# Differential attention: the mean of two softmax maps re-queued, and its outputs summed in PSUM by three products

## The chip, the cores and the metric

The kernel runs as one launch on one core of a Trainium2 chip. The metric is the device time of that core in microseconds (us), lower is better. Five engines work side by side on their own in-order queues: TensorE (PE in the profile, with PEld for its weight loads), VectorE (DVE), ScalarE (ACT), GpSimd (POOL) and SyncE (SP, which here issues DMAs). SBUF is the working memory; PSUM is the accumulation memory that TensorE writes, eight banks of 512 float32 per partition.

## The reference

A decoder trunk of two layers, sequence 512, width 1024, in float32. Layer 0 has differential attention as its token mixer, layer 1 a causal pooling mixer. Around each mixer stand two SwiGLU feed-forward blocks, a cross attention into 256 memory tokens, and a layer norm after each step. Only the differential attention is touched here: 8 heads; each head has two query/key pairs of width 64 and values of width 128. Cut to what matters:

```
for each block of 128 queries i, each head h, each map c in (0, 1):
    s = q[c] @ k[c].T * scale;  s = where(kpos <= qpos, s, min)
    p[c] = softmax(s)
a = p[0] - lam * p[1]
o = a @ v
o = o * rsqrt(mean(o * o) + eps) * subln_g * (1 - lam_init)
y = concat(o over heads) @ w_o
```

## The kernel before

Float32 products are made from rounded halves: an operand x is split into `hi` (x rounded to a shorter format, a cast on ACT) and `lo = x - hi` (a subtraction on DVE), and a product is the sum of hi*hi, hi*lo and lo*hi in one PSUM bank (`mm3`, lines 210 to 212). The trunk runs stage by stage; the projections and feed-forward blocks keep TensorE in such triples.

The differential attention stage has two streams, woven by `weave`. `da_main` is the projections: for each pair of heads the values, then for each head queries and keys (lines 210 to 212 with outputs named v, q, k), with the rotary embedding on DVE and POOL (`da_rope`, L1083 to L1086, output `rt`) and the splits of queries (`qk`, L1096 and L1097) and keys (`qk`, `low`, L1110 to L1112). `da_side` is the attention of heads whose projections are ready, one tile of 128 queries (i = 0..3) of a head at a time. A step s of `da_side` does, for tiles that lag behind each other:

- `da_scores` of tile s: for both maps two products of 128 x 128(i+1) into a bank `sc` (L1125, L1126); then, with priority, on DVE the masked copy `p` and its minimum (L1131, called mask below: one instruction and the read of its accumulator) and on ACT the exponential with its row sum (L1134).
- `da_mix` of tile s-1: on DVE the reciprocal of a row sum (L1143), the factor `cf` (L1144) and `p0 + cf*p1` (L1145), called the mix below. The normalisation of `p0` is left to the end, where the mean square takes it up.
- `da_turn` of tile s-2: transposes of `p` on TensorE (L494, output `pt`), then hi and lo of the result, `a` (L125 on ACT, L126 on DVE).
- `da_out` of tile s-3: the product with the values. For each block j of 128 keys, the hi of `a` is the stationary operand and the hi and lo of the values, side by side, are the moving one (L1166, 256 columns); the lo of `a` meets the hi of the values (L1167, 128 columns). So a bank `po` holds, for two tiles, two sums of 128 columns each that have still to be added: a copy on ACT (L1172), and an addition on DVE (L1173), give `o`. Two Square activations on ACT (L1176) read `o`, and write their elementwise result, which nobody reads, back into the bank `po`; their accumulators are the sums of squares `sq`. After a head's last tile POOL makes the factor `f` (L1183 to L1186), later ACT scales `o` (L1192), TensorE transposes it (L494, `pt<-ident,o`), and it is split into `oT` (L130, L131) for the output projection (`ps`).

The banks for `sc`, `pt` and `po` come in turn from three pools of two (`aux`): a new tile waits until the last reader or writer of the tile that had its bank is done.

The order on each engine is set at build time by a scheduler that takes instructions by priority as their inputs come ready in its own estimate; `high_priority()` lets an instruction go ahead of others, and `after(...)`/`issue_after` places one behind a named instruction in the queue, with no wait on it. On the chip each queue then runs strictly in that order.

Of the kernel before, what the change touches and what calls it, by code (L numbers as in the profile page):

```python
# [12 lines left out]
AF = mybir.ActivationFunctionType  # L13
ALU = mybir.AluOpType
# [3 lines left out]
P = 128  # L18
# [91 lines left out]
class Trunk:  # L110
# [80 lines left out]
    def mm(self, name):  # L191
        return self.mmp.tile([P, S], F32, tag="mm", name=name)
# [922 lines left out]
    def da_scores(self, st, i):  # L1115

        nc = self.nc
        q, k, n = st["q"], st["k"], (i + 1) * P
        qi, kn = slice(i * P, n), slice(0, n)
        mx, rc, cf = self.small("mx"), self.small("rc", (P, 1)), self.small("cf", (P, 1))  # L1120
        sm = st["sm"][:, i]
        sc = [self.aux("sc")[:, :n] for m in range(2)]
        mm = nc.tensor.matmul
        for m in range(2):
            mm(sc[m], q[m][:, qi], k[0][m][:, kn], start=True, stop=False)  # L1125
            mm(sc[m], q[m][:, qi], k[1][m][:, kn], start=False, stop=True)  # L1126
        p = [self.tmp("p")[:, :n] for m in range(2)]
        with self.tc.high_priority():
            for m in range(2):
                least = mx[:, m : m + 1]  # L1130
                nc.vector.tensor_tensor_reduce(  # L1131
                    p[m], sc[m], self.mask[:, S - n :], -1.0, -NEG, ALU.add, ALU.min, least
                )
                nc.scalar.activation(  # L1134
                    p[m], p[m], AF.Exp, bias=least, scale=-1.0, accum_out=sm[:, m : m + 1]
                )
        st["m", i] = p, sm, rc, cf

    def da_mix(self, st, i):

        nc = self.nc
        p, sm, rc, cf = st.pop(("m", i))
        nc.vector.reciprocal(rc, sm[:, 1:2])  # L1143
        nc.vector.scalar_tensor_tensor(cf, sm[:, 0:1], self.nlam, rc, ALU.mult, ALU.mult)  # L1144
        nc.vector.scalar_tensor_tensor(p[0], p[1], cf, p[0], ALU.mult, ALU.add)  # L1145
        st["p", i] = p[0]

    def da_turn(self, st, i):
# [8 lines left out]
    def da_out(self, st, i):  # L1157
        nc = self.nc
        if i == 0:
            st["o"], st["sq"] = self.tmp("o", (P, NT, P)), self.small("sq", (P, NT))  # L1160
        if i % 2 == 0:
            st["po"] = self.aux("po").rearrange("p (i s e) -> p i s e", i=2, s=2)
        a, o, po, mm = st.pop(("a", i)), st["o"], st["po"], nc.tensor.matmul
        for j in range(i + 1):
            v = st["v"][j][:, st["h"] % 2]
            mm(po[:, i % 2], a[0][:, j], v, start=j == 0, stop=False)  # L1166
            mm(po[:, i % 2, 0], a[1][:, j], v[:, 0], start=False, stop=j == i)  # L1167
        if i % 2 == 0:
            return
        o2 = o[:, i - 1 : i + 1]  # L1170
        with self.tc.high_priority():
            nc.scalar.copy(o2, po[:, :, 1])  # L1172
            nc.vector.tensor_tensor(o2, o2, po[:, :, 0], ALU.add)  # L1173
        sq = st["sq"]
        for i in range(i - 1, i + 1):
            nc.scalar.activation(  # L1176
                po[:, 0, 0], o[:, i], AF.Square, scale=float(P**-0.5), accum_out=sq[:, i : i + 1]
            )
        if i < NT - 1:
            return  # L1180

        f, G, s0 = self.small("f", (P, NT)), nc.gpsimd, st["sm"][:, :, 0]
        G.tensor_scalar(f, s0, EPS, None, ALU.mult)  # L1183
        G.tensor_tensor(f, f, s0, ALU.mult)
        G.tensor_tensor(f, f, sq, ALU.add)
        G.tensor_tensor(f, f, self.mhalf, ALU.pow)  # L1186
        st["f"] = f
# [446 lines left out]

    def mixer(self, layer, ln):
        if layer == 0:
            bufs = dict(low=4, rt=2, a=4, p=6, o=2, qk=8, _x=0, v=4, oT=11, mask=1)
            with self.other_pools(), self.phase_pool(("v", "v"), "rt", **bufs):
                self.diff_attention(layer, ln)
            self.close_side()  # L1640
        else:
            self.later = ExitStack()
            self.later.enter_context(self.stage_pools(4, dict(raw=2), ("wh", "wl", "mem", "p", "raw")))
            self.to_w(self.later)
            self.kvp = self.later.enter_context(self.pool("kv"))
            bufs = dict(p=4, pw=1, gb=2, _x=0, pooled=16, sq=1)
            with self.phase_pool(("gb", "gb"), "sq", **bufs):
                side = self.pool_mixer(layer, ln)
                with self.tc.high_priority():
                    self.load_memory()  # L1650
                w = self.a["xa_wkv"][layer]
                raws = [self.raw_cols(w, c) for c in (0, D)]
                self.pool_bias()
                next(side)
                self.kv, self.keys, self.kv_bufs = [], [], 10
                self.weave(self.early_kv(layer, ln, 2, raws), side, 850, 8500)
            self.close_side()
# [46 lines left out]
```

## Time and profile before

| What | Value |
|---|---|
| time, median of 3 runs | 1921.71 us (1919.52 to 1921.93) |
| profiled execution, time and span | 1921.52 us, span 1919.7 us |
| granted TensorE clock, mean | 0.999 |
| busy share of the span | PE 99%, weight loads 91%, DVE 81%, ACT 53%, POOL 17% |
| attention stage, about 355 to 580 us of the span | 225 us: PE busy 217.8, DVE 188.4, ACT 144.9 |

In the trace an output tile and its inputs are written as `out<-in`; `xN` counts instructions. The time behind a bar or in brackets is how long the engine stood idle before the instruction, and for whom it waited. The ends of matmuls are modelled, their starts are recorded, so the cost of a matmul is read best from one start to the next. 128x256 behind a matmul is its output: 128 partitions by 256 columns, the columns being those of the moving operand.

### The profile page before, as it was taken

The page shows a single profiled execution, that of the slowest core. Times are in us where ns is not written, and L with a number is a line of the kernel's source. Part 1 is how long each engine was busy: PE and PEld are TensorE (multiplying, and loading weights), DVE is VectorE, ACT ScalarE, POOL GpSimd, SP SyncE. Part 2 cuts the span into 40 slices and gives each one's busy share as a digit, 9 for nine tenths or more (in the row PEclk, how much of TensorE's full clock was granted, in tenths as well). Part 3 has the DMA queues.
Part 4 walks back from the last instruction along what each step waited for, and adds up shares of the span by engine and source line. Part 5 has one row for each costly group of instructions (what it writes and reads, how often), then busy time and mean ns, then how long its engine had stood idle before and what let it go on. Part 6 is the DMA issues. An engine that isn't in the chain of part 4 may idle for free.

```text
span 1919.7 us, 32489 instructions
## 1 busy us (share of the span) xinstructions
PE 1895.9 (99%) x13072; PEld 1738.2 (91%) x13072; DVE 1563.6 (81%) x2264; ACT 1023.4 (53%) x1580; POOL 319.8 (17%) x278
## 2 busy tenths in 40 slices
PE   9999999999999999999999999999999999999998
PEld 8999998888878888999998999999899889999997
DVE  7888889888867558889888988898787568998886
ACT  6555454567755435645554655455455436555552
POOL 3112121111210002221220311212130012111210
PEclk9999999999999999999999999999999999999999
DMA  9978772322224327987785587878344437877861
GB/s 250 213 173 179 175 140 78 91 66 88 66 88 154 110 66 195 180 179 162 144 192 180 108 180 164 183 164 183 108 132 132 133 87 162 174 168 167 186 133 55
DMA packets 246743, 277.96 MB, mean 145 GB/s; under 512 B 8256, under 2 KB 212544, under 8 KB 246592
## 3 DMA queue, kind: packets, MB, share of 16 engines
q0 software_dynamic: 92928, 92.29, 31.4%
q1 hardware_dynamic: 153664, 183.59, 29.8%
q8 instruction: 103, 1.69, 0.4%
q14 instruction: 48, 0.39, 0.1%
HBM read 273.75 MB, written 2.10 MB: 144 GB/s over the span
## 4 chain that ended last, share of the span: by engine, by line
PE 78%; DVE 13%; ACT 4%; DMA 2%; issue 2%; POOL 1%; SPq 0%; DVEq 0%; ACTq 0%; POOLq 0%
PE x L210 7%; PE x L211 7%; PE x L212 7%; PE z L212 4%; PE z L210 4%; PE z L211 4%; PE ps L210 4%; PE ps L212 4%; PE ps L211 4%; PE px L210 2%; PE px L212 2%; PE px L211 2%; PE y L212 2%; PE xq L210 1%; PE xq L211 1%
## 5 line engine op out<-in xcount | busy, mean ns | idle before, releaser
L685 POOL DMA_DIRECT2D ra<-in_ffn_w_in_dram x132 | 170.7, 1313 | 982.8 <-DVE wl L692 808.9
L690 ACT CAST wh<-ra 128x1024 fp32r<-128x1024 f32 x176 | 185.1, 1054 | 207.5 <-PE x L211 66.5
L692 DVE TENSOR_TENSOR wl<-ra,wh 128x1024 fp32r<-128x1024 f32 x176 | 213.9, 1220 | 67.1 <-ACT wh L690 66.4
L210 PE MATMUL x<-xe,wh 128*128 128x256 f32 x704 | 195.0, 277 | 0.0
L211 PE MATMUL x<-xe,wh 128*128 128x256 f32 x704 | 194.8, 277 | 0.0
L690 ACT CAST wh<-rc 128x1024 fp32r<-128x1024 f32 x132 | 138.9, 1053 | 104.9 <-PE x L211 40.4
L212 PE MATMUL x<-xe,wl 128*128 128x256 f32 x704 | 194.8, 277 | 0.0
L125 ACT CAST wh<-b 128x1024 fp32r<-128x1024 f32 x112 | 117.8, 1052 | 128.9 <-PE x L211 65.1
L692 DVE TENSOR_TENSOR wl<-rc,wh 128x1024 fp32r<-128x1024 f32 x132 | 159.8, 1218 | 26.8 <-ACT wh L690 26.8
L126 DVE TENSOR_TENSOR wl<-b,wh 128x1024 fp32r<-128x1024 f32 x112 | 136.6, 1220 | 40.2 <-ACT wh L125 40.2
L210 PE MATMUL x<-xh,wh 128*128 128x256 f32 x536 | 148.7, 277 | 0.0
L211 PE MATMUL x<-xl,wh 128*128 128x256 f32 x536 | 148.4, 277 | 0.0
L212 PE MATMUL x<-xh,wl 128*128 128x256 f32 x536 | 148.4, 277 | 0.0
L211 PEld LDWEIGHTS x<-xe,wh 128*128 128x128 f32 x704 | 132.5, 188 | 1.4
L210 PEld LDWEIGHTS x<-xe,wh 128*128 128x128 f32 x704 | 132.2, 188 | 1.3
L212 PEld LDWEIGHTS x<-xe,wl 128*128 128x128 f32 x704 | 132.2, 188 | 0.0
L126 DVE TENSOR_TENSOR wl<-raw,wh 128x1024 fp32r<-128x1024 f32 x64 | 83.0, 1300 | 42.4 <-ACT wh L125 41.6
L211 PEld LDWEIGHTS x<-xl,wh 128*128 128x128 f32 x536 | 100.9, 188 | 0.7
L210 PEld LDWEIGHTS x<-xh,wh 128*128 128x128 f32 x536 | 100.6, 188 | 0.7
L212 PEld LDWEIGHTS x<-xh,wl 128*128 128x128 f32 x536 | 100.6, 188 | 0.0
L125 ACT CAST wh<-raw 128x1024 fp32r<-128x1024 f32 x64 | 66.5, 1049 | 59.3 <-PE xq L211 21.0
L210 PE MATMUL z<-xe,wh 128*128 128x256 f32 x352 | 97.5, 277 | 0.0
(450 smaller groups left out, 6329.1 us busy)
## 6 DMA issues: line engine op xcount, KB each, us to landing
ra<-in_ffn_w_in_dram POOLq DMA_DIRECT2D x132, 512.0 KB, 7.0
rc<-in_ffn_w_in_dram SPq DMA_DIRECT2D x88, 512.0 KB, 5.7
b<-in_ffn_w_out_dram SPq DMA_DIRECT2D x76, 512.0 KB, 4.7
ra<-in_ffn_w_in_dram SPq DMA_DIRECT2D x44, 512.0 KB, 4.7
rc<-in_ffn_w_in_dram POOLq DMA_DIRECT2D x44, 512.0 KB, 8.0
raw<-in_xa_wkv_dram SPq DMA_DIRECT2D x16, 1024.0 KB, 5.4
raw<-in_da_w_qkv_dram SPq DMA_DIRECT2D x16, 512.0 KB, 5.3
raw<-in_xa_wq_dram SPq DMA_DIRECT2D x8, 1024.0 KB, 5.1
```

Of the source, the lines that this page charges most:

```text
L125: self.nc.scalar.copy(hi, src),
L126: self.nc.vector.tensor_sub(lo, src, hi.bitcast(F32)),
L210: mm(out, w[0], x[0], start=start, stop=False, skip_group_check=again)
L211: mm(out, w[0], x[1], start=False, stop=False, skip_group_check=again)
L212: self.last_mm = mm(out, w[1], x[0], start=False, stop=stop, skip_group_check=again)
L685: nc.gpsimd.dma_start(t, source(*block), accum_op=ALU.add)
L690: hi = nc.scalar.copy(v[0], raw)
L692: lo = nc.vector.tensor_sub(v[1], raw, v[0].bitcast(F32))
```

## The change

Three edits to the attention stage.

1. `da_mix` gets priority, and is placed in the queue behind the last mask of the tile that was just scored (`self.masked`, the second L1131 of tile s, while the mix is that of tile s-1).
2. `da_out` sums everything in one place: hi*hi, hi*lo and lo*hi are three products of 128 columns into the same 128 columns of `po` (new lines L1167, L1168, L1169, the first two with the same stationary operand). The bank holds the finished `o`; the ACT copy moves both tiles at once, and the DVE addition is gone.
3. The Square activations write to a small SBUF tile `squares`, and no longer to `po`.

```diff
@@ da_scores
         with self.tc.high_priority():
             for m in range(2):
                 least = mx[:, m : m + 1]
-                nc.vector.tensor_tensor_reduce(
+                self.masked = nc.vector.tensor_tensor_reduce(
                     p[m], sc[m], self.mask[:, S - n :], -1.0, -NEG, ALU.add, ALU.min, least
                 )
@@ da_mix
-        nc.vector.reciprocal(rc, sm[:, 1:2])
-        nc.vector.scalar_tensor_tensor(cf, sm[:, 0:1], self.nlam, rc, ALU.mult, ALU.mult)
-        nc.vector.scalar_tensor_tensor(p[0], p[1], cf, p[0], ALU.mult, ALU.add)
+        with self.after([self.masked]), self.tc.high_priority():
+            nc.vector.reciprocal(rc, sm[:, 1:2])
+            nc.vector.scalar_tensor_tensor(cf, sm[:, 0:1], self.nlam, rc, ALU.mult, ALU.mult)
+            nc.vector.scalar_tensor_tensor(p[0], p[1], cf, p[0], ALU.mult, ALU.add)
@@ da_out
         if i % 2 == 0:
-            st["po"] = self.aux("po").rearrange("p (i s e) -> p i s e", i=2, s=2)
+            st["po"] = self.aux("po")[:, : 2 * P].rearrange("p (i e) -> p i e", i=2)
         a, o, po, mm = st.pop(("a", i)), st["o"], st["po"], nc.tensor.matmul
         for j in range(i + 1):
             v = st["v"][j][:, st["h"] % 2]
-            mm(po[:, i % 2], a[0][:, j], v, start=j == 0, stop=False)
-            mm(po[:, i % 2, 0], a[1][:, j], v[:, 0], start=False, stop=j == i)
+            mm(po[:, i % 2], a[0][:, j], v[:, 0], start=j == 0, stop=False)
+            mm(po[:, i % 2], a[0][:, j], v[:, 1], start=False, stop=False)
+            mm(po[:, i % 2], a[1][:, j], v[:, 0], start=False, stop=j == i)
...
         with self.tc.high_priority():
-            nc.scalar.copy(o2, po[:, :, 1])
-            nc.vector.tensor_tensor(o2, o2, po[:, :, 0], ALU.add)
-        sq = st["sq"]
+            nc.scalar.copy(o2, po)
+        sq, squares = st["sq"], self.tmp("squares", (P, P))
         for i in range(i - 1, i + 1):
             nc.scalar.activation(
-                po[:, 0, 0], o[:, i], AF.Square, scale=float(P**-0.5), accum_out=sq[:, i : i + 1]
+                squares, o[:, i], AF.Square, scale=float(P**-0.5), accum_out=sq[:, i : i + 1]
             )
@@ mixer
-            bufs = dict(low=4, rt=2, a=4, p=6, o=2, qk=8, _x=0, v=4, oT=11, mask=1)
+            bufs = dict(low=4, rt=2, a=4, p=6, o=2, qk=8, _x=0, v=4, oT=11, mask=1, squares=1)
```

How the rows stand now, at three places. First TensorE, where the first tile of the first head meets its values (one block of keys); before:

```order
L212 MATMUL v<-wh,xl 128x256
L1166 MATMUL po<-v,a 128x256
L1167 MATMUL po<-v,a 128x128
L210 MATMUL v<-wh,xh 128x256
L211 MATMUL v<-wl,xh 128x256
```

And at the same place of the changed kernel:

```order
L212 MATMUL v<-wh,xl 128x256
L1167 MATMUL po<-v,a 128x128
L1168 MATMUL po<-v,a 128x128
L1169 MATMUL po<-v,a 128x128
L210 MATMUL v<-wh,xh 128x256
L211 MATMUL v<-wl,xh 128x256
```

Two matmuls have become three; there are 80 such places (8 heads, 1+2+3+4 blocks of keys), and on the rest of TensorE's queue the order is the same, but for the last head's transposes of `o`, which moved up by two or three matmuls, and the order of a few projections just behind them.

Second, DVE around the mix of the third tile of the fifth head (384 columns), about 481 to 488 us in the trace; before:

```order
L1086 TENSOR_TENSOR rt<-rt 128x512
L1173 TENSOR_TENSOR o<-o,po 128x256
L1144 SCALAR_TENSOR_TENSOR cf<-sd,nlam,rc 128x1
L126 TENSOR_TENSOR wl<-raw,wh 128x1024
L1131 ISA p,mx<-sc,mask 128x512
L1131 ISA mx 128x1
L1131 ISA p,mx<-sc,mask 128x512
L1131 ISA mx 128x1
L1097 SCALAR_TENSOR_TENSOR qk<-rt,qk 64x512 x2
L1145 SCALAR_TENSOR_TENSOR p<-p,cf 128x384
L126 TENSOR_TENSOR a<-pt,a 128x256
```

The same stretch now:

```order
L1086 TENSOR_TENSOR rt<-rt 128x512
L126 TENSOR_TENSOR wl<-raw,wh 128x1024
L1131 ISA p,mx<-sc,mask 128x512
L1131 ISA mx 128x1
L1131 ISA p,mx<-sc,mask 128x512
L1131 ISA mx 128x1
L1144 RECIPROCAL rc<-sd 128x1
L1097 SCALAR_TENSOR_TENSOR qk<-rt,qk 64x512
L1145 SCALAR_TENSOR_TENSOR cf<-sd,nlam,rc 128x1
L1097 SCALAR_TENSOR_TENSOR qk<-rt,qk 64x512
L1146 SCALAR_TENSOR_TENSOR p<-p,cf 128x384
L126 TENSOR_TENSOR a<-pt,a 128x256
```

The mix stands where it stood, behind both masks and both query splits; the addition is gone, and the reciprocal, which stood four rows above the first one shown, now stands behind the masks.

Third, DVE around the mix of the last tile of the sixth head (512 columns), about 507 to 513 us; the masks of 128 columns are those of the next head's first tile. Before:

```order
L126 TENSOR_TENSOR wl<-raw,wh 128x1024
L1131 ISA p,mx<-sc,mask 128x128
L1131 ISA mx 128x1
L1131 ISA p,mx<-sc,mask 128x128
L1131 ISA mx 128x1
L1086 TENSOR_TENSOR rt<-rt 128x512
L1144 SCALAR_TENSOR_TENSOR cf<-sd,nlam,rc 128x1
L1143 RECIPROCAL rc<-sd 128x1
L1145 SCALAR_TENSOR_TENSOR p<-p,cf 128x512
L126 TENSOR_TENSOR a<-pt,a 128x384
L1111 TENSOR_TENSOR low<-rt,qk 64x512 x2
L1173 TENSOR_TENSOR o<-o,po 128x256
```

And now:

```order
L1131 ISA p,mx<-sc,mask 128x128
L1131 ISA mx 128x1
L1086 TENSOR_TENSOR rt<-rt 128x512
L1131 ISA p,mx<-sc,mask 128x128
L1131 ISA mx 128x1
L1144 RECIPROCAL rc<-sd 128x1
L126 TENSOR_TENSOR wl<-raw,wh 128x1024
L1145 SCALAR_TENSOR_TENSOR cf<-sd,nlam,rc 128x1
L1111 TENSOR_TENSOR low<-rt,qk 64x512
L126 TENSOR_TENSOR a<-pt,a 128x384
L1146 SCALAR_TENSOR_TENSOR p<-p,cf 128x512
```

A weight split, a key split and a split of `a` have come between the second mask and the mix. At the first tile of the first head, the mix moved up instead: it stood behind both masks of 384 columns, and now stands between them.

## The prediction

> **What bounds the kernel now.** I read the page's head first, then the busy times of the attention stage, then TensorE's waits inside that stage.
>
> ```profile
> span 1919.7 us, 32489 instructions
> PE 1895.9 (99%) x13072; PEld 1738.2 (91%) x13072; DVE 1563.6 (81%) x2264; ACT 1023.4 (53%) x1580; POOL 319.8 (17%) x278
> ...
> 355.00:580.00 225.00, 217.82 (x1261) 187.35 (x1260) 188.37 (x457) 144.86 (x376) 38.50 (x50) 1.00 0.25 77
> ```
>
> TensorE is the bound of the whole program, and of the stage that the change touches: 217.8 of 225 us, DVE second with 188.4, ACT third with 144.9. The granted clock is full, so a matmul added there costs its time at full clock. Nothing behind the stage waits for a time of its own, so what the stage loses or wins reaches the end.
>
> What TensorE still has to win is its waits in that stretch (us in total, times, longest):
>
> ```profile
> PE pt L494 <- DVE p L1145: 2.6, 2, 1.4
> PE sc L1125 <- ACT po L1176: 1.5, 2, 0.8
> PE pt L494 <- ACT o L1192: 1.1, 1, 1.1
> PE sc L1125 <- ACT qk L1112: 0.9, 2, 0.7
> PE po L1167 <- DVE a L126: 0.6, 1, 0.6
> PE ps L210 <- DVE X L362: 0.3, 1, 0.3
> PE po L1166 <- ACT a L125: 0.2, 1, 0.2
> ```
>
> That is 7.2 us in 10 waits. A wait costs a little more than the idle time shown, since the pipeline has to start again:
>
> ```profile
> 375.34 0.28 PE L212 MATMUL v<-wh,xl 128*128 128x256 f32 x1
> 376.99 0.33 PE L494 MATMUL pt<-ident,p 128*128 128x128 f32 x1 [1.37 <-DVE p L1145]
> ```
>
> The transpose would have followed 0.12 us behind the matmul (the step of 256 columns, below), so at 375.46; it came at 376.99: 1.53 lost for 1.37 shown. With 0.16 more for each of the ten, all the waits are worth 8.8 us. No change of order can return more.
>
> **The third product.** Starts of the old pair, and of the only 128-column products that follow each other now, the scores of a head's first tile:
>
> ```profile
> 471.37 0.33 PE L1166 MATMUL po<-v,a 128*128 128x256 f32 x1
> ...
> 471.60 0.34 PE L1166 MATMUL po<-v,a 128*128 128x256 f32 x1
> ...
> 506.33 0.28 PE L212 MATMUL v<-wh,xl 128*128 128x256 f32 x1
> 506.45 0.22 PE L1125 MATMUL sc<-qk 128*128 128x128 f32 x1
> 506.51 0.28 PE L1126 MATMUL sc<-low,qk 128*128 128x128 f32 x1
> 506.62 0.27 PE L1125 MATMUL sc<-qk 128*128 128x128 f32 x1
> 506.73 0.28 PE L1126 MATMUL sc<-low,qk 128*128 128x128 f32 x1
> 506.84 0.34 PE L210 MATMUL v<-wh,xh 128*128 128x256 f32 x1
> ```
>
> The old pair steps by 0.23 us: 384 columns in the time of two matmuls of 256. The scores step by 0.11 after the first: a product of 128 columns takes nearly the step of 256 (506.33 to 506.45, 0.12), because each brings its own load of the stationary operand, and only the first one's load hides behind a longer matmul. Three of them step by 0.33 to 0.34, so each block of keys costs 0.11 more; 80 blocks (8 heads of 1+2+3+4) give 8.6 us, on the path. The ends: at 0.06 a product (506.45 to 506.51) three would take 0.18, and the change would save 0.05 x 80 = 4 us; at half the old pair, 0.115, it costs 9.2. Between them I take 0.11, since it is three steps of the same kind in a row, against one that hides behind its neighbour. The two products that share a stationary operand load it twice, as L210 and L211 do with wh: the page has as many loads as matmuls, 13072.
>
> [...]
>
> **The addition and the squares.** These rows give what is removed on DVE and ACT:
>
> ```profile
> L1173 DVE TENSOR_TENSOR o<-o,po x16: 406/414/422, 389.5 to 555.8; 128x256 f32<-128x256 f32 x16
> ACT po L1176 <- DVE o L1173: 11.9, 12, 2.0
> DVE rc L1143 <- ACT p L1134: 11.4, 13, 2.6
> L1176 ACT ACTIVATE po<-o x32: 256/282/283, 390.4 to 556.6; 128x128 f32<-128x128 f32 x32
> L1192 ACT ACTIVATE o<-o,f x32: 385/392/406, 403.3 to 559.4; 128x128 f32<-128x128 f32 x32
> ```
>
> DVE loses 16 x 0.414 = 6.6 us of work, ACT up to 11.9 us of waiting for it, and DVE up to 11.4 us of standing at the reciprocal for the exponentials, since those are long done once the next masks are through. None of it is TensorE's time: it returns only what stands in the list of waits. The squares get slower by writing to SBUF: L1192, SBUF to SBUF, takes 0.39 against 0.28, so at most 0.11 x 32 = 3.5 us of ACT, under the waiting that goes; it shows only behind the last head, twice, 0.2 us.
>
> **Which waits return.** Two waits of TensorE are for a bank that the squares hold. The first:
>
> ```profile
> 480.34 0.38 ACT L1172 COPY o<-po 128x256 f32<-128x256 f32 x1
> ...
> 483.76 0.18 ACT L1176 ACTIVATION_READ_ACCUMULATOR po<-o 128x1 f32 x1
> 484.00 0.33 PE L1125 MATMUL sc<-qk 128*128 128x128 f32 x1 [0.79 <-ACT po L1176]
> ```
>
> The bank will be free when the copy ends, at 480.72 and not at 483.94. So this wait goes, and the second one like it. But what is late next is the mix on DVE:
>
> ```profile
> 479.37 0.17 DVE L1143 RECIPROCAL rc<-sd 128x1 f32<-128x1 f32 x1 [0.44 <-ACT p L1134]
> 482.28 0.41 DVE L1173 TENSOR_TENSOR o<-o,po 128x256 f32<-128x256 f32 x1
> 486.65 0.62 DVE L1145 SCALAR_TENSOR_TENSOR p<-p,cf 128x384 f32<-128x384 f32 x1
> 487.32 0.44 PE L494 MATMUL pt<-ident,p 128*128 128x128 f32 x2 [1.22 <-DVE p L1145]
> ```
>
> In the new order the mix is still behind the same masks and query splits. It comes earlier by the addition and the 0.44 of standing, 0.85. Both waits together are worth 2.3 (0.79 and 1.22, and twice 0.16). Of this 0.85 returns, and another 0.9 covers third products: the three tiles multiplied by their values just before have 3, 4 and 1 blocks of keys, 8 x 0.11, and run while DVE is the later one anyway. So 1.7 returns and some 0.6 stays. The second bank wait returns 0.8.
>
> The waits for `qk` and for `a` (0.9 and 0.8 us, four waits, 2.4 with the restarts) stand behind DVE and ACT when these stood for each other; I take them as gone.
>
> The first mix now stands ahead of the second mask of 384 columns:
>
> ```profile
> 376.10 0.55 DVE L1131 CUSTOM_DVE_ANT_0 p<-sc,mask 128x384 f32<-128x384 f32 x1
> 376.58 0.35 DVE L1145 SCALAR_TENSOR_TENSOR p<-p,cf 128x128 f32<-128x128 f32 x1
> ```
>
> It starts 0.48 earlier, and 1.05 of the 1.53 stays: no values have been multiplied by then, so no third product covers it. The waits for the scaled `o` (1.1) and for X (0.3), behind the last head, stay: that chain loses the addition and gains 0.2 of squares, but its transposes have moved up by two matmuls. I add 0.2 there.
>
> Returned: 1.7 + 0.8 + 2.4 + 0.5 = 5.4.
>
> **What the new order adds.** The mix now waits in the queue behind masks that wait for TensorE's scores. Its readers, the transposes, stand behind the scores of one tile more, so there is room. The tightest is the last tile of the sixth head:
>
> ```profile
> L126 DVE TENSOR_TENSOR wl<-raw,wh 128x1024 fp32r<-128x1024 f32 x64 | 83.0, 1300 | 42.4 <-ACT wh L125 41.6
> ...
> 510.50 0.28 DVE L1131 CUSTOM_DVE_ANT_0 p<-sc,mask 128x128 f32<-128x128 f32 x1
> 511.61 0.73 DVE L1145 SCALAR_TENSOR_TENSOR p<-p,cf 128x512 f32<-128x512 f32 x1
> 512.26 0.55 DVE L126 TENSOR_TENSOR a<-pt,a 128x384 fp32r<-128x384 f32 x1
> 512.73 0.68 DVE L1111 TENSOR_TENSOR low<-rt,qk 64x512 fp32r<-64x512 f32 x1
> 513.12 0.38 PE L494 MATMUL pt<-ident,p 128*128 128x128 f32 x2
> ```
>
> From the end of the masks (510.78) to the transposes are 2.3 us. In the new order a weight split (1.3 in the mean), `low` 0.68, `a` 0.55 and the mix 0.73 stand there, 3.3, and the reciprocal and the factor with some 0.4: late by up to 1.4. The weight split stood ahead of the masks before, though, so the masks come that much sooner unless TensorE's scores hold them. From nothing to 1.4 here, and the like at two other ends of heads: 0 to 3 us; I take 0.7, nearer the low end, because DVE has less work ahead of it by then.
>
> **The sum.** 8.6 - 5.4 + 0.2 + 0.7 = +4.1 us on the profiled execution's 1921.5 (span 1919.7 and 1.8 around it): 1925.6. The median of the runs, 1921.7, is 0.2 above that execution; I say 1925.8.
>
> **The rivals.** (A) The forecast: third products on the path, half of them paid by waits that go; 1924 to 1928. For it: 99% busy and steps of 0.11. Chance 0.52. (B) The waits go almost wholly, 7 of 8.8 us, because DVE and ACT stop standing for each other (11.4 and 11.9 us), and no new one comes: 8.6 - 7 = +1.6, 1923.3. Against it: the first wait and the last head's keep some 2.8 of the 8.8, unless the shorter chain there also helps. Chance 0.22. (C) The mix behind the masks becomes the wait: it eats the 1.7 and 0.5 of the mix's own waits and adds 1 to 3 at the ends of heads: +7 to +10, 1929 to 1932. It decides once a mask comes later than 2.3 us ahead of the transposes at several heads. Chance 0.18. (D) The other side: the load of a stationary operand hides. This asks for steps well under 0.085 us; at 0.06 it is -4 - 4.5, near 1913. Against it are three steps of 0.11 in one block. [...] Chance 0.08.
>
> A measurement of this kernel can tell about 0.2%, 3.8 us, from no change: 1917.9 to 1925.6. Faster: most of D, 0.06. Same: B, something over four tenths of A, the rest of D: 0.46. Slower: the rest of A, and C: 0.48. The likeliest case by itself has 1924 to 1928. The range takes in B's lower part and most of C: 1921 to 1931.
>
> **What would show it.** After the change: L1167, L1168 and L1169 step by 0.11 us; the waits of `sc` for `po` are gone; the reciprocals wait no more for ACT; TensorE's waits in the stage add up to 2.5 to 4 us; the stage is 4 us longer. It is wrong if the three products step by 0.28 or less, or if waits of `pt` for the mix add up to more than 4 us.

## The result and the profile after

The changed kernel takes 1923.99 us in the median (1921.27 to 1926.79), the kernel before 1920.28 on the same chip (1919.29 to 1922.49). The ratio is 1.0017, with a 95% interval of 1.0011 to 1.0023: 3.3 us slower, 2.1 to 4.4. So the change is clear of noise, and just smaller than the 0.2% up to which the prediction spoke of "same". The forecast was 1925.8 in a range of 1921 to 1931, that is 4.1 more than the 1921.7 from which it started, with "same" at 0.46 and "slower" at 0.48.

The head of the page, after:

```profile
span 1922.2 us, 32637 instructions
PE 1902.5 (99%) x13152; PEld 1745.6 (91%) x13152; DVE 1558.4 (81%) x2248; ACT 1025.0 (53%) x1580; POOL 321.8 (17%) x278
```

The 80 products are there (13152 against 13072), and their loads with them; DVE has lost 16 instructions and 5.2 us. The profiled execution took 1923.98 us against 1921.52, 2.46 more. Nearly all of this lies in the attention stage. It can be cut out of the trace at two matmuls that both kernels have: the first score product, and the first product with the memory behind the stage. The tiles' rows (shortest, median and longest ns, then first and last start), of before:

```profile
L1125 PE MATMUL sc<-qk x64: 218/331/470, 370.0 to 542.7; 128*128 128x128 f32 x16, 128*128 128x256 f32 x16, 128*128 128x384 f32 x16, 128*128 128x512 f32 x16
L210 PE MATMUL pk<-mem0h,wh x32: 276/281/363, 583.8 to 1491.4; 128*128 128x256 f32 x32
```

And of after:

```profile
L1125 PE MATMUL sc<-qk x64: 218/317/397, 369.0 to 543.6; 128*128 128x128 f32 x16, 128*128 128x256 f32 x16, 128*128 128x384 f32 x16, 128*128 128x512 f32 x16
L210 PE MATMUL pk<-mem0h,wh x32: 276/277/368, 585.4 to 1492.3; 128*128 128x256 f32 x32
```

From 370.0 to 583.8 are 213.8 us; from 369.0 to 585.4 are 216.4. So the stage is 2.6 us longer. Below, each kernel's stage is split in two: the *steps*, its matmuls laid end to end at the steps seen in undisturbed rows (0.112 us for 128 columns, 0.456 ns a column for 256 to 512), and the *excess*, all the rest: waits, restarts, slow steps. Before has 204.0 of steps and 9.8 of excess, after 212.6 and 3.8. By this count the third products cost 8.6, and 6.0 came back.

The steps of the new products, in TensorE's timeline of after:

```profile
470.60 0.22 PE L1167 MATMUL po<-v,a 128*128 128x128 f32 x1
470.65 0.27 PE L1168 MATMUL po<-v,a 128*128 128x128 f32 x1
470.76 0.27 PE L1169 MATMUL po<-v,a 128*128 128x128 f32 x1
470.88 0.28 PE L1167 MATMUL po<-v,a 128*128 128x128 f32 x1
...
471.21 0.27 PE L1167 MATMUL po<-v,a 128*128 128x128 f32 x1
```

From 470.88 to 471.21 three products pass, 0.11 each; only the step behind the first, whose load began at 470.37 under the longer matmul ahead of it (470.36), is 0.05 by these rows. What TensorE still waits for, from 355 to 590 us (the last row lies behind the stage, and is 1.0 in before too):

```profile
PE pt L494 <- DVE p L1146: 1.8, 3, 0.9
PE pt L494 <- ACT o L1193: 1.1, 1, 1.1
PE pk L211 <- DVE mem0l L126: 1.0, 1, 1.0
```

Inside the stage 2.9 us in 4 waits are left of 7.2 in 10. Both waits for the bank are gone, and those for `qk`, for `a` and for X. The three waits for the mix, and the place at the end of the sixth head:

```profile
375.36 0.33 PE L494 MATMUL pt<-ident,p 128*128 128x128 f32 x1 [0.76 <-DVE p L1146]
...
469.44 0.30 PE L494 MATMUL pt<-ident,p 128*128 128x128 f32 x1 [0.16 <-DVE p L1146]
...
486.23 0.33 PE L494 MATMUL pt<-ident,p 128*128 128x128 f32 x1 [0.86 <-DVE p L1146]
...
512.24 0.28 PE L212 MATMUL v<-wh,xl 128*128 128x256 f32 x1
512.52 0.30 PE L494 MATMUL pt<-ident,p 128*128 128x128 f32 x1
```

The first mix wait fell from 1.37 to 0.76, the one of the fifth head from 1.22 to 0.86 (and the 0.79 for the bank ahead of it is gone). At the sixth head's end the transpose comes 0.28 behind the projection in place of 0.12, so the mix is 0.16 late there. And the reciprocals no longer stand for the exponentials, 0.8 in place of 11.4 us (the splits of `a` on DVE stand longer for ACT in return, 9.0 in place of 3.6):

```profile
DVE rc L1144 <- ACT p L1134: 0.8, 1, 0.8
```

The squares, now to SBUF, take 0.31 in place of 0.28 us:

```profile
L1177 ACT ACTIVATE squares<-o x32: 293/311/313, 389.2 to 558.1; 128x128 f32<-128x128 f32 x32
```

### The profile page after: what moved, and what is told of

It reads as the page before. It is cut to its first block, busy times and chain, and to the rows that moved or that the text cites. A ratio compares the mean times of both kernels' runs of the same rounds, so it can differ in the third digit from the quotient of the medians.

```text
span 1922.2 us, 32637 instructions
## 1 busy us (share of the span) xinstructions
PE 1902.5 (99%) x13152; PEld 1745.6 (91%) x13152; DVE 1558.4 (81%) x2248; ACT 1025.0 (53%) x1580; POOL 321.8 (17%) x278
## 4 chain that ended last, share of the span: by engine, by line
PE 81%; DVE 12%; ACT 2%; DMA 2%; issue 1%; POOL 1%; SPq 0%; DVEq 0%; ACTq 0%; POOLq 0%
PE x L210 7%; PE x L211 7%; PE x L212 6%; PE z L212 4%; PE z L211 4%; PE z L210 4%; PE ps L210 4%; PE ps L212 4%; PE ps L211 4%; PE px L210 2%; PE px L212 2%; PE px L211 2%; PE y L212 2%; PE pz L212 2%; PE pz L211 2%; PE pz L210 2%
```

## The experiments

All ratios are against the kernel before, on the same chip, with 95% intervals. "Stage" is from the first score product to the first `pk`, in the one profiled execution of each kernel; the steps in it are counted, the excess is the rest.

| kernel | ratio | stage | steps | excess |
|---|---|---|---|---|
| before | 1 | 213.8 | 204.0 | 9.8 |
| after | 1.0017 [1.0011, 1.0023] | 216.4 | 212.6 | 3.8 |
| e1, order of the mix alone | 0.9996 [0.9987, 1.0004] | 213.2 | 204.0 | 9.1 |
| e2, squares in SBUF alone | 1.0002 [0.9993, 1.0011] | 214.0 | 204.0 | 9.9 |
| e3, three products alone | 1.0026 [1.0015, 1.0037] | 219.9 | 212.6 | 7.3 |
| e4, order and squares | 1.0000 [0.9991, 1.0009] | 213.2 | 204.0 | 9.2 |
| e5, after with two products | 0.9979 [0.9971, 0.9988] | 209.9 | 203.6 | 6.2 |
| e6, after with four products | 1.0053 [1.0040, 1.0065] | 223.7 | 221.6 | 2.2 |
| e8, e4 with priority only | 0.9999 [0.9990, 1.0008] | 212.8 | 204.0 | 8.8 |
| e9, after with priority only | 1.0028 [1.0018, 1.0038] | 219.7 | 212.6 | 7.1 |
| e10, e4 with a rotary sum on POOL | 1.0046 [1.0033, 1.0058] | 222.1 | 204.0 | 18.0 |
| e11, after with a rotary sum on POOL | 1.0067 [1.0054, 1.0080] | 227.7 | 212.6 | 15.1 |
| e12, e4 with the factor on POOL | 1.0023 [1.0013, 1.0034] | 216.5 | 204.0 | 12.5 |
| e13, three products in half the tiles | 0.9997 [0.9987, 1.0008] | 213.7 | 206.6 | 7.1 |

Two things limit what a row of this table says. The excess of e2, e3, e9, e10 and e11 holds some 1.7 us each in which TensorE's clock ran at a half after a wait (told at the end); the profiled executions of the others have no such stretch in the stage. And the order of the queues is made anew for each build, so an edit can also move instructions that it does not name. In this stage before and e2 have the same order on every engine, and so have e1 and e4; between e4 and e5 the order differs at many places on DVE and ACT.

### The three edits apart: e1, e2, e3, e4

e1 is the kernel before with the mix behind the masks:

```diff
-                nc.vector.tensor_tensor_reduce(
+                self.masked = nc.vector.tensor_tensor_reduce(
...
-        nc.vector.reciprocal(rc, sm[:, 1:2])
+        with self.after([self.masked]), self.tc.high_priority():
+            nc.vector.reciprocal(rc, sm[:, 1:2])
...
```

> Edit 1 alone: the mix with priority behind the next tile's masks; outputs by two products and the addition, squares into the bank, as before. Theory (the DVE order pays with waits): the reciprocals no longer stand for the exponentials (11.4 us of DVE before), so the waits of TensorE for the mix, for qk and for a shrink; the two waits for the bank that the squares hold (1.5 us) stay. 1.5 to 3.5 us faster than before. Rival (the mix is now late, behind masks that wait for scores): new waits of the transposes for the mix at the ends of heads, no change or up to 3 us slower.

e2 is the kernel before with the squares in SBUF:

```diff
-        sq = st["sq"]
+        sq, squares = st["sq"], self.tmp("squares", (P, P))
...
-                po[:, 0, 0], o[:, i], AF.Square, scale=float(P**-0.5), accum_out=sq[:, i : i + 1]
+                squares, o[:, i], AF.Square, scale=float(P**-0.5), accum_out=sq[:, i : i + 1]
```

> Edit 3 alone: the squares write to SBUF, all else as before. Theory: the bank is free at the end of the addition, not of the second square, about 1.2 us sooner; both waits of the scores for the bank (0.79 and 0.67 us) go or nearly go, but the mix behind one of them is then late: 0.5 to 1.5 us faster. Rival (slower squares, 0.31 us in place of 0.28, delay ScalarE): no change or slower by less than 1 us.

e3 is the kernel before with the three products and without the addition; the squares still go to the bank:

```diff
-            mm(po[:, i % 2], a[0][:, j], v, start=j == 0, stop=False)
-            mm(po[:, i % 2, 0], a[1][:, j], v[:, 0], start=False, stop=j == i)
+            mm(po[:, i % 2], a[0][:, j], v[:, 0], start=j == 0, stop=False)
+            mm(po[:, i % 2], a[0][:, j], v[:, 1], start=False, stop=False)
+            mm(po[:, i % 2], a[1][:, j], v[:, 0], start=False, stop=j == i)
...
-            nc.scalar.copy(o2, po[:, :, 1])
-            nc.vector.tensor_tensor(o2, o2, po[:, :, 0], ALU.add)
+            nc.scalar.copy(o2, po)
...
-                po[:, 0, 0], o[:, i], AF.Square, scale=float(P**-0.5), accum_out=sq[:, i : i + 1]
+                po[:, 0], o[:, i], AF.Square, scale=float(P**-0.5), accum_out=sq[:, i : i + 1]
```

> Edit 2 alone: three products of 128 columns, the addition gone, the squares into the bank (its first tile's columns), the mix as before. Theory (the third product is on the path, and waits cover part of it): 80 x 0.111 = 8.9 us less the old step, 8.6 us, on TensorE; the addition's going returns some 2 to 4 us of waits: 4.5 to 6.5 us slower than before. Rival (the third product is nearly covered by waits of TensorE whatever the order of DVE): less than 3 us slower.

e4 is e1 and e2 together, which is the changed kernel with the old pair of products and the addition; against the changed kernel:

```diff
-            mm(po[:, i % 2], a[0][:, j], v[:, 0], start=j == 0, stop=False)
-            mm(po[:, i % 2], a[0][:, j], v[:, 1], start=False, stop=False)
-            mm(po[:, i % 2], a[1][:, j], v[:, 0], start=False, stop=j == i)
+            mm(po[:, i % 2], a[0][:, j], v, start=j == 0, stop=False)
+            mm(po[:, i % 2, 0], a[1][:, j], v[:, 0], start=False, stop=j == i)
...
-            nc.scalar.copy(o2, po)
+            nc.scalar.copy(o2, po[:, :, 1])
+            nc.vector.tensor_tensor(o2, o2, po[:, :, 0], ALU.add)
```

> Edits 1 and 3 without 2: the mix behind the masks and the squares to SBUF, but two products and the addition. Theory (what was gained is the order of DVE and ACT, what was lost is the third product): the waits mostly go without the 8.6 us being paid; but no third product covers what DVE is late by, so some waits stay: 3 to 5 us faster than before, 6 to 8 faster than the changed kernel. Rival (the waits went because TensorE itself got slower by the third products, and the order has little part in it): within 1.5 us of before.

Order and squares, alone or together, move nothing that can be measured (0.9996, 1.0002, 1.0000), so what was expected of e1 and e4 did not come, and their rivals held; e2 is too near to decide. The waits of TensorE in e4 show why:

```profile
PE pt L494 <- DVE p L1146: 5.7, 3, 2.9
...
PE sc L1125 <- ACT qk L1112: 0.5, 2, 0.3
```

The waits for the bank and for `a` are gone, and those for `qk` fell from 0.9 to 0.5. But the waits for the mix rose from 2.6 to 5.7, two of them at the places that the prediction had looked at:

```profile
485.77 0.33 PE L494 MATMUL pt<-ident,p 128*128 128x128 f32 x1 [2.95 <-DVE p L1146]
...
512.77 0.30 PE L494 MATMUL pt<-ident,p 128*128 128x128 f32 x1 [2.00 <-DVE p L1146]
```

DVE's standing did not go either, it moved from the reciprocals to the splits of `a`. Before:

```profile
DVE a L126 <- ACT a L125: 3.6, 5, 2.2
```

In e4, where the reciprocals no longer stand:

```profile
DVE a L126 <- ACT a L125: 10.8, 12, 2.3
```

This makes a part of both long waits, for there the mix stands behind such a split in DVE's queue. At the fifth head:

```profile
484.76 0.43 DVE L126 TENSOR_TENSOR a<-pt,a 128x256 fp32r<-128x256 f32 x1 [0.67 <-ACT a L125]
485.10 0.61 DVE L1146 SCALAR_TENSOR_TENSOR p<-p,cf 128x384 f32<-128x384 f32 x1
```

At the end of the sixth head the split waited longer, because ACT's half of it stood in the queue behind scalings of `o` that waited for POOL's factor:

```profile
508.73 0.99 ACT L1193 ACTIVATE o<-o,f 128x128 f32<-128x128 f32 x3 [3.37 <-POOL f L1187]
...
511.41 0.56 DVE L126 TENSOR_TENSOR a<-pt,a 128x384 fp32r<-128x384 f32 x1 [2.33 <-ACT a L125]
511.88 0.74 DVE L1146 SCALAR_TENSOR_TENSOR p<-p,cf 128x512 f32<-128x512 f32 x1
```

In e1 the waits for the mix are 4.9, in e2 3.6. TensorE's waits in e2:

```profile
PE pt L494 <- DVE p L1145: 3.6, 2, 2.3
...
PE sc L1125 <- ACT qk L1112: 0.9, 2, 0.7
PE po L1167 <- DVE a L126: 0.6, 1, 0.6
```

In e2 the squares no longer hold the bank. At the fifth head the 0.79 for the bank is gone, and the mix behind it is waited for 1.03 longer; the second bank wait (0.67) is gone for good. All waits of the stage are 6.7 in place of 7.2, and the half clock took 1.7. So most of what these two edits removed came back under another name, and they alone return nothing.

e3 has the full price of the products, and is slower by 5.0 us on 1920, with 2 either way, as expected. It returns 2.5 of 9.8 (excess 7.3), though it has no order; some 1.7 of what stays is one disturbance of the clock, told at the end. Both waits for the bank are gone here too, with the squares still in it.

### The products counted: e5, e6

e5 leaves out one product, so `o` lacks hi of the probabilities times the low half of the values; e6 has the same term twice. Nothing else in the source differs from the changed kernel; in the queues a few instructions of DVE and ACT have other places. e5:

```diff
-            mm(po[:, i % 2], a[0][:, j], v[:, 1], start=False, stop=False)
```

> The changed kernel without the second of its three products (hi of a by lo of the values is left out, so the output misses that term). Theory (VectorE sets the time of two stretches of the stage, and the third product is partly covered there): TensorE gets 80 x 0.111 = 8.9 us less work than in the changed kernel, but waits come back, mostly of the transposes for the mix: 4.5 to 6.5 us faster than the changed kernel, 1 to 3 us faster than before. Rival (the third product is paid in full, the waits that went are due to the order): 8 to 9 us faster than the changed kernel, 4.5 to 5.5 us faster than before.

e6:

```diff
             mm(po[:, i % 2], a[0][:, j], v[:, 1], start=False, stop=False)
+            mm(po[:, i % 2], a[0][:, j], v[:, 1], start=False, stop=False)
```

> The changed kernel with the second product issued twice (so that term is counted twice). Theory: what can be covered is mostly covered by the third product already (2.9 us of waits are left, 1.1 of them behind the last head, 0.8 before the first values): the fourth product costs 8 to 9 us more than the changed kernel. Rival (waits go on covering it): 5 to 7 us more.

e5 has the order, the squares, and no addition, and pays for no third product. It is 0.21% faster than before, 4.0 us with 1.7 either way, between what theory and rival gave; its stage is 3.3 us shorter than that of e4, which has edits 1 and 3 too. The first `pk` of e5, which began its scores at 369.1:

```profile
L210 PE MATMUL pk<-mem0h,wh x32: 276/278/366, 578.9 to 1486.8; 128*128 128x256 f32 x32
```

The way from before to after, in the stage: order and squares -0.6, the addition taken away -3.3 (0.4 of it steps, since a product of 256 columns has become one of 128), the third product +6.5; sum +2.6. Of the excess, 0.6, 3.0 and 2.4 returned, 6.0 in all. By the ratios: 0.00, -0.21, +0.38%, that is 7.3 us on 1920 for the third product, with 2 either way. On another way the parts come out otherwise: from e3, which has the products and no addition, to after, edits 1 and 3 are worth 3.5 of the stage, 1.7 of it the half clock. The third product costs 9.0 of steps (80 of 0.112), and 2.4 of it runs while TensorE would have waited: the excess falls from 6.2 to 3.8. The fourth costs 9.0 of steps again, 7.4 of the stage and 0.36%, 6.9 us with 2.6 either way: by the stage 1.6 of it are still covered. I had expected 8 to 9 for it, with nothing left to cover it; the rival's 5 to 7 is nearer, though the ratios alone don't rule out the 8 to 9.

Where the cover lies is seen at the mix of the fifth head. e5's row there:

```profile
483.95 0.33 PE L494 MATMUL pt<-ident,p 128*128 128x128 f32 x1 [1.78 <-DVE p L1146]
```

And e6's, with no wait:

```profile
489.02 0.49 PE L494 MATMUL pt<-ident,p 128*128 128x128 f32 x3
```

The wait is 2.95 in e4, 1.78 in e5, 0.86 in after and nothing in e6. From e5 to after it falls by 0.92, and the last 0.86 goes with the next product: 8 products of 0.11, the three tiles' blocks of keys just ahead, are 0.88. From e4 to e5, where the addition (0.41) goes, it falls by 1.17. Most of this is order: in e5, as in before and after, the mix stands ahead of the split of `a`, and did not wait for it.

```profile
483.27 0.62 DVE L1146 SCALAR_TENSOR_TENSOR p<-p,cf 128x384 f32<-128x384 f32 x1
484.62 0.42 DVE L126 TENSOR_TENSOR a<-pt,a 128x256 fp32r<-128x256 f32 x1 [0.73 <-ACT a L125]
```

In e4 the query split ahead of both ended at 484.09, and the mix began 1.0 later, at 485.10. The 2.00 at the end of the sixth head is gone in e5 as well, with two products only: the scalings of `o` stand further ahead in ACT's queue there, and wait no longer. So the 3.0 from e4 to e5 are the addition together with the order that the build chose without it; no run has the one without the other.

### The place in the queue: e8, e9

e8 is e4, and e9 the changed kernel, with the mix put by priority alone:

```diff
-        with self.after([self.masked]), self.tc.high_priority():
+        with self.tc.high_priority():
```

> Edits 1 and 3 without 2, and the mix with priority only, not behind the next masks: it stands ahead of them again. Theory (with two products VectorE is late at two places, and there the mix waits for its turn behind masks and query splits): the waits of the transposes for the mix, 5.7 us with the mix behind the masks, fall to 1 to 2.5 us, but the reciprocals stand for the exponentials again (some 5 to 11 us of VectorE), which brings waits for qk and for a: 0 to 2.5 us faster than before. Rival (the total of VectorE's work and standing sets the time, wherever the mix stands): within 1 us of before, with waits of 8 to 9 us under other names.

> The changed kernel with the mix on priority only, not behind the next masks. Theory (with three products TensorE is late nearly everywhere, so the place of the mix hardly counts): within 1.5 us of the changed kernel. Rival (being behind the masks is what lets VectorE go on without standing for the exponentials): 2 to 4 us slower than the changed kernel, with reciprocals that wait for ScalarE.

With two products the place makes no difference (0.9999 against e4's 1.0000). The waits of e8 have other names, though. Its TensorE and DVE:

```profile
PE po L1167 <- ACT a L125: 1.0, 1, 1.0
PE pt L494 <- DVE p L1146: 0.9, 1, 0.9
...
DVE rc L1144 <- ACT p L1134: 12.8, 14, 2.6
```

The waits for the mix fell from 5.7 to 0.9, and the splits of `a` on DVE and ACT became late. With three products the place behind the masks may be worth something, but not clear of noise: 1.0017 against 1.0028, 2.1 us with 2.2 either way, and against e3's 1.0026, whose mix has neither priority nor place. The stage of e9 is 3.3 us longer than that of after. In e9 `a` is late for the products by 1.9, and the reciprocals stand for 18.4 us:

```profile
DVE rc L1144 <- ACT p L1134: 18.4, 17, 2.5
```

About 1.7 of those 3.3 us are slow steps at the half clock behind that wait for `a`, not the wait itself.

### Is it DVE's work, or its chain? e10, e11, e12, e13

If DVE's sum of work set the waits, 16 rotary additions (0.68 us each, 10.9 in all) moved to POOL should return more than the addition of `o` did. e10 does this in e4, e11 in the changed kernel:

```diff
-        nc.vector.tensor_tensor(t1, t1, t2, ALU.add)
+        nc.gpsimd.tensor_tensor(t1, t1, t2, ALU.add)
```

> Edits 1 and 3 without 2 (two products and the addition), and the last addition of the rotary embedding (L1086, 16 x 0.68 us) on GpSimd in place of VectorE. Theory (TensorE waits for VectorE's total work in two stretches): VectorE gets 10.9 us less, more than the 6.6 of the addition that edit 2 takes away, and TensorE no more: 2 to 5 us faster than before. Rival (the chain from the projections through the rotary embedding to the scores is what counts, and GpSimd makes it 0.6 us longer each time): within 1 us of before or slower, with longer waits of the scores for qk.

> The changed kernel with the last addition of the rotary embedding on GpSimd. Theory: of the changed kernel's 2.9 us of waits only the one for the mix at the fifth head (0.9) and the small one (0.2) can still go, so at most 1 us faster than the changed kernel, 2 to 3.5 us slower than before. Rival: the longer rotary chain makes new waits for qk, 1 to 3 us slower than the changed kernel.

e12 is e4 with the reciprocal and the factor on POOL:

```diff
-            nc.vector.reciprocal(rc, sm[:, 1:2])
-            nc.vector.scalar_tensor_tensor(cf, sm[:, 0:1], self.nlam, rc, ALU.mult, ALU.mult)
+            nc.gpsimd.tensor_tensor(rc, sm[:, 1:2], self.minus, ALU.pow)
+            nc.gpsimd.tensor_tensor(cf, sm[:, 0:1], self.nlam, ALU.mult)
+            nc.gpsimd.tensor_tensor(cf, cf, rc, ALU.mult)
```

> Edits 1 and 3 without 2, and the factor of the mix made on GpSimd (power -1 and two multiplications, about 1.5 us there) in place of the reciprocal and the factor on VectorE (32 x 0.38 us). Theory: VectorE gets 12 us less, GpSimd 46 more of the 200 in which it works 40: 2 to 4 us faster than before. Rival (GpSimd's queue now stands for the exponentials, with the rotary products behind): no change or slower, with waits for qk.

e13 has three products for the first two tiles of a head (24 blocks of keys), and two products and the addition for the other two:

```diff
+            if three:
+                mm(po[:, i % 2], a[0][:, j], v[:, 0], start=j == 0, stop=False)
+                mm(po[:, i % 2], a[0][:, j], v[:, 1], start=False, stop=False)
+                mm(po[:, i % 2], a[1][:, j], v[:, 0], start=False, stop=j == i)
+            else:
...
```

> The changed kernel with three products for the first two tiles of a head only (24 blocks), two products and the addition for the other two (56 blocks). Theory (a third product costs about 0.09 us net a block, and an addition that goes returns about 0.25 us of waits by making VectorE earlier): 24 x 0.09 = 2.2 us paid, 8 x 0.25 = 2 returned: within 1 us of before. Rival (the additions of the first two tiles are those that make VectorE late): 1.5 to 2.5 us faster than before.

The sum fell as a theory. With less work on DVE, e10 is slower than e4 by 0.46%, e11 slower than after by 0.50% (9.6 us, where even the rival had expected 1 to 3); some 1.7 us of the profiled execution of each are the half clock. The rotary sum in e10, and the waits for the mix:

```profile
L1086 POOL TENSOR_TENSOR rt<-rt x16: 1267/1627/2237, 361.0 to 518.7; 128x512 f32<-128x512 f32 x16
...
PE pt L494 <- DVE p L1146: 6.9, 5, 2.0
PE sc L1125 <- ACT qk L1112: 1.8, 4, 1.0
```

Each addition now takes 1.6 us in place of 0.68, in the chain from the projection to the scores. ACT stands 31.9 us for it, in place of 17.2 in e4, and TensorE's waits for `qk` rose from 0.5 in e4 to 1.8, and those for the mix to 6.9 (8.0 in e11). e12 takes two short operations off DVE and is 0.23% slower than before. TensorE waits no more for the mix, but for the splits of `a`, and these stand 15.0 us for ACT in place of 10.8:

```profile
PE pt L494 <- DVE a L126: 2.4, 2, 1.6
PE po L1169 <- DVE a L126: 1.9, 2, 1.1
```

e13 pays 24 x 0.11 = 2.6 of steps and gets 2.0 of it back (excess 9.2 in e4, 7.1 here): 0.9997, as expected. Its mix waits 3.9 us in all, between e4's 5.7 and after's 1.8. So less work on DVE alone does not shorten the waits. That the length of a chain through the queues sets them fits e10 to e12, but each of these takes work off DVE and lengthens a chain at once, so it is not shown apart. Of the versions that compute the whole product, none is measurably faster than the kernel before.

## Why the prediction was right

The forecast was +4.1 us. Over all runs the kernel is 3.3 slower, 2.1 to 4.4, which takes in the 4.1; the one profiled execution is 2.46 slower, 1.6 less than forecast. By its steps:

**The third product** held: 0.11 a step as forecast, so 8.6 in all by the count of steps; from e5 to the changed kernel and from there to e6, one product more costs 7.3 and 6.9 us net. e5 adds that 2.4 of the products' time ran under waits, where the prediction had counted 0.9, at one head alone.

**The addition and the squares.** That DVE's 11.4 us of standing at the reciprocals are none of TensorE's time was right: in e4 they are gone, and its ratio is 1.0000. They were not saved, though: the standing moved to the splits of `a`. But the step called the addition's 6.6 us no time of TensorE's, outside the listed waits. Taking it out, with the order that the build then chose, returned 3.0 of excess, from e4 to e5, half of all that came back. The squares' 0.31 lies near the low end of 0.28 to 0.39. The wait behind the last head is 1.1 as before, where 0.2 more was forecast.

**Which waits return** held in size: 5.4 forecast, and after the 0.9 set against it, 4.5 net; 6.0 measured net. Place by place: the first mix wait 0.6 (0.5 forecast); both bank waits, `qk` and `a` gone, as forecast; the fifth head's mix left at 1.0 with its restart, 0.6 forecast. There the part for the third products was right, 0.9 forecast and 0.92 measured from e5 to after. X's 0.3 was forecast to stay, and went. About 1.0 us more of the excess of before stands in no wait that is listed (9.8 less 7.2 and ten restarts of 0.16), and it went too.

What was wrong in this step is the reason given for part of it. "It comes earlier by the addition and the 0.44 of standing" took the two as independent amounts, and the `qk` and `a` waits as gone because the engines stop standing for each other. With the reciprocals' standing gone and the addition kept, the same wait is 2.95 (e4), longer than the 1.22 and 0.79 of before together, since the mix had come to stand behind a split of `a` that waits for ACT; and `qk` waits on. The returns came with the addition's going, partly by the queue orders that the build chose without it, and with the cover of the third products, not from edits 1 and 3 alone. That the forecast of 5.4 came so near is in part luck.

**What the new order adds** was set at 0.7, of 0 to 3. It is 0.16 shown at 469.44 and 0.16 of lateness at 512.52, with a restart some 0.5. A late mix does come: at 512.77 in e4 it is 2.00 us, in the very place that the prediction priced at up to 1.4, and 1.79 and 1.77 in e1 and e13. But its cause is not rival C's. In e4 the second mask ended at 507.00, 5.8 us ahead of the transposes, and not less than 2.3. What came late was the split of `a` ahead of the mix, held up by ACT's standing for POOL's factor (3.37 us). Without the addition the scalings stand elsewhere, and the wait is gone, in e5 even without third products.

**The rivals.** By all runs (+3.3, 2.1 to 4.4) the result lies nearer to A's +4.1 than to B's +1.6; by the stage of the one profiled execution it lies between them: 6.0 returned where A had 4.5 and B 7. The waits left in the stage, 2.9, are within the 2.5 to 4 forecast, the mix's 1.8 are under the 4 that would have refuted it, and the stage is 2.6 us longer where 4 was forecast. D is out: behind the first product of a tile, no step is under 0.10 (0.11 at most places).

What stays open: how much of the 6.0 belongs to which edit. e3 has the removal without the order and e4 the order without the removal; e3's excess is 7.3, of which 1.7 is the half clock, e4's 9.2 and after's 3.8. Beyond the sum of the two, 1.2 us then return in one execution of each, and by the ratios it cannot be told from nothing. Nor was an edit tried with the queues' order held as it was.

## What to carry to other kernels

A matmul of 128 columns that brings its own load of the stationary operand costs 0.11 us here, nearly as much as one of 256 (0.12), so a wide product and an addition elsewhere are cheaper for TensorE than narrow products summed in PSUM (here 0.23 us a block of keys against 0.33), unless the addition sits on the chain that TensorE waits for. Then count both: the steps added, and what the shorter chain and the longer matmul stream return, which here was 6.0 of 8.6. Here an order changed in the in-order queues moved most of the waits to the next reader; list the waits by name before and after, and compare their sum, not the one that was aimed at. And where a build makes the order anew, compare the queues too: from e4 to e5 much of the gain lay in instructions that no edit named.

## What the hardware showed that was not expected

After a wait of only 1.66 us, TensorE's granted clock fell to a half, 0.50. In e3:

```profile
488.88 0.33 PE L1166 MATMUL po<-v,a 128*128 128x128 f32 x1 [1.66 <-ACT a L125]
...
491.01 0.63 PE L211 MATMUL q<-xl,wh 128*128 128x512 f32 x1
491.44 0.63 PE L212 MATMUL q<-xh,wl 128*128 128x512 f32 x1
```

And the same stretch by windows (the column after the engines' busy times is the granted clock):

```profile
488.00:490.00 2.00, 0.82 (x4) 0.68 (x5) 1.89 (x8) 1.33 (x5) 0.00 (x0) 0.93 0.01 2
490.00:492.00 2.00, 2.00 (x8) 1.71 (x8) 1.21 (x5) 2.00 (x7) 0.00 (x0) 0.50 0.00 0
492.00:494.00 2.00, 2.00 (x10) 1.67 (x9) 1.63 (x4) 0.26 (x1) 1.29 (x1) 0.72 0.00 0
```

Products of 512 columns step by 0.43 there in place of 0.23. What is missing from a clock of 1.00 in the three windows is 0.14, 1.00 and 0.56 us, 1.7 in all, which is a clock of 0.50 for 3.4 us. The same came behind a wait of 1.85 in e9 (0.50 from 490 to 492), behind one of 2.25 in e2 (0.50 from 486 to 488), and once each in e10 and e11, near waits of 1.99 and 3.26. The mean granted clock of these five profiled executions is 0.998, that of the others 0.999. It did not come near 2.95 and 2.00 in e4, where the clock stayed at 1.00. It costs about 1.7 us each time, which no list of waits shows. A wait of 1.66 had a fall behind it and one of 2.95 had none, so the length of the wait alone does not decide; what does was not shown, and no run was made to vary it.

On POOL, an addition of 128x512 took 1.27, 1.63 and 2.24 us (shortest, median, longest of 16 in e10), against 0.68 of the same on DVE.
